# Four weight tiles interleaved column by column, so that the stationary operand is read with a stride of four elements

## The chip, the cores and the metric

The kernel runs on one core of a Trainium2 chip. The metric is the device time of one execution in microseconds (us), lower is better. A difference of 0.2% (4.5 us) is about what a measurement of this kernel can tell from no change.

## The reference

One block of a transformer in float32, for 272 tokens (16 learned "meta" tokens ahead of 256 others), width 2048. Three sublayers are added to the residual stream `h`; the output is `h` without the meta tokens:

```python
h = h + 0.5 * rmsnorm(swiglu(rmsnorm(h), ffn1_w_gu, ffn1_w_down))    # 2048 -> 2 x 5632 -> 2048
h = h + rmsnorm(hybrid_mixer(rmsnorm(h), w_in, pool_w, w_pool_o, w_q_b, w_kv_b, w_mla_o, w_out))
h = h + 0.5 * rmsnorm(swiglu(rmsnorm(h), ffn2_w_gu, ffn2_w_down))
```

The mixer is the sum of two gated branches: window means over the tokens (`w_pool_o`), and attention of 16 heads with low-rank queries, keys and values (`w_q_b`, `w_kv_b`, `w_mla_o`), followed by `w_out`. After the first feed-forward the meta tokens matter as keys, values and window inputs only, so the later products have 256 tokens.

Nearly all of the work is products of an activation with a weight matrix that is used once.

## The kernel before

**Layout.** Activations lie transposed: features on the 128 partitions, tokens along the free dimension. A product is computed as tiles of its transposed output, [128 output features, 272 or 256 tokens] in one PSUM bank: the weight tile [128, 128] is the stationary operand of the tensor engine, and the activation's tile [128, tokens] is the moving one, accumulated over the 128-row tiles `k` of the input (16 of them for width 2048, 44 for 5632).

**Precision.** A float32 is split into two parts of 12 bits, `hi` and `lo`, both of type float32r (4 bytes). A float32 product is made of three products: hi by hi, hi by lo, lo by hi. `mm3` (lines 211 to 215) issues them as three multiplications of 272 or 256 columns: weight `hi` by activation `hi` (L213), weight `hi` by activation `lo` (L214), weight `lo` by activation `hi` (L215). Where there are 256 tokens, `mm_wide` (lines 217 to 221) takes activation `hi` and `lo` side by side: weight `hi` by 512 columns (L219), then weight `lo` by 256 (L221). Each multiplication instruction comes with its own load of the stationary operand (a LDWEIGHTS, shown as PEld), also where L213 and L214 have the same weights.

**The weight stream.** The host lays out all weights as one stream of [128, 128] tiles in the order of their use; the order is collected by a dry run of `build`. In the class `Weights`, `load` (L79) fetches chunks of CH = 8 tiles, [128, 1024] float32, 512 KB, on the SP queue, RAW = 5 chunks ahead. `divide` splits PT = 4 tiles at a time, [128, 512]: ScalarE writes `hi` (L92), VectorE writes `lo` = raw - `hi` (L93), into HL = 6 buffers each. `take` hands out the next tile's `hi` and `lo`: tile `j` of four is the columns `j*128` to `j*128+127` of the [128, 512] buffer, so a weight load reads 128 float32 side by side on each partition.

Only the value projection takes four tiles at once, `take(t0, t1, t2, t3)`: there the activation is the stationary operand and the weights `wh`, `wl` [128, 512] are the moving one (`proj_v`, L603 to L608).

**Stages, in order of time.** First feed-forward (L = 272 tokens, `mm3`; 88 output tiles of 16 `k`, then 16 of 44); the mixer's input product (`mm3`), its 32 gate tiles (`mm_wide`); attention, head by head, with `mm3` of 256 or 272 columns for queries, keys and `w_pool_o` (tiles `q`, `k`, `qr`, `po`), and with multiplications that have no weights (scores `s` L621 and L622, transposes `pt` L653, values `o`); `w_mla_o` with the activation `o`, and `w_out` with the activation `y` (`mm_wide`); the second feed-forward with activations `x` and `a` (`mm_wide`). The last of 16 output tiles of some products is `mm3` with 256 columns. `w<-...` are the first tiles of a product, computed side by side, `m<-...` the rest. `warm` (L232) are multiplications that only keep the tensor engine's clock up; `rms` are those of the norms (L243 with a moving operand of one column; L254 with a stationary operand that is one column repeated 128 times by a stride of zero).

Of the kernel before, what the change touches and what calls it, by code (L numbers as in the profile page):

```python
# [14 lines left out]
P = 128  # L15
# [3 lines left out]
R = 256  # L19
# [8 lines left out]
CH, PT = 8, 4  # L28
RAW, HL = 5, 6
WARM = (3, 7)  # L30
GAP, SPACE = 4, 12

G_F1PRE, G_F1POST, G_MPRE, G_MPOST, G_F2PRE, G_F2POST = (16 * i for i in range(6))
# [5 lines left out]


class Nothing:
    """Stands in for the builder's objects while the order of the weights is collected."""

# [16 lines left out]
class Weights:  # L60
    """The weights as one stream of [128, 128] tiles in the order of their use; each chunk of CH
    tiles is loaded ahead, and split, PT tiles at a time, into two parts of 12 bits, which together
    are the float32."""

# [32 lines left out]
    def take(self, *tiles):  # L97
        """The next tiles of the stream, side by side."""
        n = len(tiles)
        room = PT - len(self.order) % PT  # L100
        if room < n:
            self.order += [None] * room
        at = len(self.order)
        self.order += tiles
        if self.plan is None:
            return Nothing(), Nothing()
        assert self.plan[at : at + n] == list(tiles)
        p, j = divmod(at, PT)
        self.load((p + HL - 1) * PT // CH + RAW)
        self.divide(p + min(HL - 1, p // 2 + 2))  # L110
        for _ in tiles:
            self.tick()
        hi, lo = self.split[p]
        s = slice(j * P, (j + n) * P)
        return hi[:, s], lo[:, s]


class Later:
    """Work that is issued some steps of the weights' stream later, so that an engine isn't held
    by what another one has yet to do."""  # L120

# [3 lines left out]
    def __call__(self, *steps):  # L125
        """steps: pairs of a delay after the one before, and what to run then."""
        at = self.now
        for delay, run in steps:
            at += delay
            self.due.append((at, run))  # L130
        self.due.sort(key=lambda d: d[0])
# [11 lines left out]
def build(nc, tc, ctx, hT, wsrc, gains_d, const_d, tables_d, out, order):  # L143
# [7 lines left out]
    parts = ctx.enter_context(tc.tile_pool(name="parts", bufs=HL))  # L151
# [4 lines left out]
    later = Later()  # L156
# [14 lines left out]

# [1 line left out]
    h = slot3(KD, L, F32, "h")  # L173
# [3 lines left out]
    zero = temp("zero")  # L177
# [5 lines left out]
    ident, ones = const[:, :P], const[:, P:]  # L183
    eps = keep.tile([P, 2], F32, tag="eps", name="eps")
    pool_e.memset(eps[:, 0:1], EPS)
    pool_e.memset(eps[:, 1:2], 4 * EPS)
    acc = keep.tile([P, L], F32, tag="acc", name="acc")
# [6 lines left out]
    class Two:  # L194
        """n tiles of T tokens in two parts of 12 bits, side by side."""

# [20 lines left out]
    def mm_wide(b, w, x, k, first, last):  # L217
        """The same with the product of the low part of x in columns of its own, from R on."""
        mm(b.rearrange("p (b c) -> p b c", b=2), w[0], x.both(k, R), start=first, stop=last,  # L219
           skip_group_check=True)  # L220
        mm(b[:, :R], w[1], x.hi(k, R), start=False, stop=last, skip_group_check=True)  # L221

    def join(b, s):
        """s: the sum of both halves of b, in two steps."""
        act(s, b[:, R:], AF.Copy)
        return GAP, lambda: dve.tensor_tensor(s, b[:, :R], s, op=ALU.add)

    def warm(n, x=ident):
        """Keeps the tensor engine's clock up while it has to wait."""
        b = bank("warm")  # L230
        for _ in range(n):
            mm(b[:, :P], x[:, :P], x[:, :P], start=True, stop=True)  # L232

# [1 line left out]
    def rms_sums(sources, T, n, half=False):  # L235
        """1 / sqrt(mean + eps), or half of it, of the tokens whose squares' sums over the
        partitions of `sources` add up to n * mean; the tokens are on partitions."""
        b = bank("rms")
        tt = (0, P, L - P)[: 3 if T == L else 2]
        m, c0 = len(tt), 400  # L240
        for i, s in enumerate(sources):
            for j, t0 in enumerate(tt):
                mm(b[:, c0 + j : c0 + j + 1], s[:, t0 : t0 + P], ones[:, :1],  # L243
                   start=i == 0 and j == 0, stop=i == len(sources) - 1, skip_group_check=True)
        sd = tmp.tile([P, 4], F32, tag="sd", name="sd", bufs=2)
        f = 4 if half else 1
        act(sd[:, :m], b[:, c0 : c0 + m], AF.Sqrt, scale=f / n, bias=eps[:, f // 4 : f // 4 + 1])
        dve.reciprocal(sd[:, :m], sd[:, :m])
        return b, sd

    def rms_spread(b, sd, T):
        """The same for all partitions, in the bank's first T columns."""
        for j, (t0, c) in enumerate(((0, 0), (P, 0), (L - P, P - NMETA))[: 3 if T == L else 2]):
            mm(b[:, t0 + c : t0 + P], sd[:, j : j + 1].to_broadcast([P, P]), ident[:, c:],  # L254
               start=True, stop=True)
# [8 lines left out]
    def squares(src, T, j, last=False):  # L264
        """Adds the squares of src to acc; the last ones stay apart, for `rms` to add."""
        if j == 0:
            act(acc[:, :T], src, AF.Square)
            return []
        s = temp("sq")
        act(s[:, :T], src, AF.Square)  # L270
        if last:
            return [s]
        pool_e.tensor_tensor(acc[:, :T], acc[:, :T], s[:, :T], op=ALU.add)  # L273
        return []
# [3 lines left out]

# [1 line left out]
    class Stream:  # L280
        """The residual stream's parts for the next products; `update` brings a tile of it up to
        date. Issued in stages that lead the products by a tile."""

# [18 lines left out]
        def scale(self):  # L302
            """The pre-norm's scales; products of the unscaled input are scaled by them."""
            b, sd = rms_sums([acc] + self.last, self.T, DM)

            def spread():
                rms_spread(b, sd, self.T)
                dve.tensor_copy(rs[:, : self.T], b[:, : self.T])
            return spread

    def products(names, n_k, x, T, wave, evac, stream=None, hooks={}, narrow=()):
        """Tiles of x @ w, transposed: the first `wave` of them side by side, then one by one."""
        wide = [T == R and i not in narrow for i in range(len(names))]
# [32 lines left out]

# [1 line left out]
    def post(names, n_k, x, T, g_post, half, wave, wait):  # L348
# [26 lines left out]

# [1 line left out]
    def ffn(x, w_gu, w_down, g_post, wait):  # L377
# [27 lines left out]

    # ================= first feed-forward =================
    warm(10, zero)
# [8 lines left out]

    # ================= mixer =================
    x = advance(t, b, L, G_MPRE)
# [15 lines left out]
    def rotate(o, src, T):  # L434
        """Rotary embedding of rows [x1, x2, x1, x2] of 32 each; o may not be src."""
        c = slice(L - T, L)
# [33 lines left out]
    def windows(j):  # L470
        """Difference of the windows' means and the input, in parts."""
        w = WINDOWS[j // 2]
        s = u[:, j, :]
# [18 lines left out]

    # columns of w_in in tiles: c_kv, k_rope twice, c_q, u_pool
    names = [("w_in", ("kv", j)) for j in range(4)] + [("w_in", ("kr", 0))]
# [57 lines left out]

# [1 line left out]
    o2 = Two(HEADS, R, "o")  # L554
# [40 lines left out]
    def proj_v(g):  # L595
        """Rows of v of four heads: tokens 0.., tokens 128.., and those from 256 on, by the high
        part of the input in rows 64.. and by the low part in rows 80.. ."""
        bs = [bank(f"v{i}") for i in range(3)]
# [47 lines left out]
    def turn(i):  # L646
        """Transposes the probabilities: keys 128.. and keys 0.. of the two times 128 queries. Of
        the first 128 queries' keys from 128 on only 16 exist, the rows below are zero; the second
        ones' keys from 256 on go to rows 64.. and again to rows 80.. of the last columns."""
        b = bank("pt")  # L650
# [49 lines left out]

# [1 line left out]
    y = Two(KD, R, "y")  # L702
# [17 lines left out]

    # ================= second feed-forward =================
    t, b = ffn(advance(t, b, R, G_F2PRE), "ffn2_w_gu", "ffn2_w_down", G_F2POST, (0, 0))
# [15 lines left out]
def columns(name, m):  # L738
    """Columns of a weight that make its tile m."""
    a = np.arange(P)  # L740
# [71 lines left out]
```

## Time and profile before

| | |
|---|---|
| median of 3 runs | 2244.52 us (2244.32 to 2246.24) |
| span of the profiled execution | 2257.5 us |
| PE (multiplications) busy | 99%, 15040 instructions |
| PEld (weight loads) busy | 91%, 15040 instructions |
| VectorE, ScalarE, GpSimd busy | 60%, 51%, 9% |
| DMA | 393.46 MB, mean 174 GB/s |

The profiled execution is 13.0 us longer than the median of the runs. PE's multiplications are pipelined: one begins while the one before it still drains, so the sum of their durations says little, and PE is busy nearly always. What a multiplication takes of PE is read from the distance between the starts of one and the next, that is, from the timeline, or from the count of instructions in a stretch of time. The same holds for PEld.

### The profile page before, as it was taken

To read this page: it belongs to the slowest core of one execution; us is meant where nothing else is said; L and a number is where in the kernel's file an instruction comes from. 1 tells how busy PE (TensorE), PEld (TensorE's weight loads), DVE (VectorE), ACT (ScalarE), POOL (GpSimd) and SP (SyncE) were. 2 spreads that over 40 slices of the span, in tenths; PEclk is the share of its full clock that TensorE was granted. 3 is DMA by queue.
4 is the path that set the end of the run, shared out by engine and by line. 5 is a ranking of instruction groups with operands and counts; after the bars stand their busy time and mean duration, and the time that the engine had idled before them with its cause. 6 is when DMAs were issued, how large, how long until landed. Compare 5 with 4: busy or idle time off the path is not lost.

```text
span 2257.5 us, 39449 instructions
## 1 busy us (share of the span) xinstructions
PE 2234.3 (99%) x15040; PEld 2062.4 (91%) x15040; DVE 1362.2 (60%) x2456; ACT 1142.5 (51%) x2273; POOL 205.4 (9%) x229
## 2 busy tenths in 40 slices
PE   9999999999999999999999999999999999999997
PEld 9999999999999999988888888888888888888886
DVE  6555555555444477766666677577666666654554
ACT  6444444444444454555544555665555555554543
POOL 2000000000000053200121111150000000000001
PEclk9999999999999999999999999999999999999999
DMA  6555555555555545566533356545655555655553
GB/s 242 178 175 174 179 172 178 177 170 177 177 169 180 175 150 168 178 190 188 173 113 122 114 169 195 186 151 186 185 188 184 188 186 186 187 191 187 187 182 117
DMA packets 109311, 393.46 MB, mean 174 GB/s; under 512 B 12288, under 2 KB 13696, under 8 KB 109120
## 3 DMA queue, kind: packets, MB, share of 16 engines
q1 hardware_dynamic: 108576, 389.19, 53.7%
q8 instruction: 118, 1.93, 0.4%
q0 software_dynamic: 400, 1.61, 0.2%
q14 instruction: 73, 0.60, 0.1%
q10 hardware_dynamic: 144, 0.13, 0.0%
HBM read 388.78 MB, written 2.10 MB: 173 GB/s over the span
## 4 chain that ended last, share of the span: by engine, by line
PE 97%; DVE 2%; issue 1%; DMA 0%; ACT 0%; SPq 0%; ACTq 0%; DVEq 0%
PE m L219 29%; PE m L221 15%; PE m L213 13%; PE m L215 12%; PE m L214 12%; PE w L219 2%; PE w L214 1%; PE w L221 1%; PE w L215 1%; PE s L622 1%; PE w L213 1%; PE po L213 1%; PE po L215 1%; PE po L214 1%; PE s L621 1%
## 5 line engine op out<-in xcount | busy, mean ns | idle before, releaser
L93 DVE TENSOR_TENSOR lo<-raw,hi 128x512 fp32r<-128x512 f32 x1472 | 1042.9, 722 | 691.7 <-ACT hi L92 686.7
L92 ACT ACTIVATE hi<-raw 128x512 fp32r<-128x512 f32 x1472 | 882.5, 625 | 393.6 <-PE m L214 283.1
L219 PE MATMUL m<-x,hi 128*128 128x512 f32 x1824 | 643.3, 398 | 0.0
L221 PE MATMUL m<-x,lo 128*128 128x256 f32 x1824 | 513.0, 281 | 0.0
L213 PE MATMUL m<-x,hi 128*128 128x272 f32 (+1 forms) x1488 | 429.6, 289 | 0.0
L215 PE MATMUL m<-x,lo 128*128 128x272 f32 (+1 forms) x1488 | 429.2, 288 | 0.0
L214 PE MATMUL m<-x,hi 128*128 128x272 f32 (+1 forms) x1488 | 428.4, 288 | 0.0
L219 PEld LDWEIGHTS m<-x,hi 128*128 128x128 f32 x1824 | 342.9, 188 | 83.2
L221 PEld LDWEIGHTS m<-x,lo 128*128 128x128 f32 x1824 | 345.0, 189 | 0.0
L214 PEld LDWEIGHTS m<-x,hi 128*128 128x128 f32 x1488 | 282.9, 190 | 0.0
L213 PEld LDWEIGHTS m<-x,hi 128*128 128x128 f32 x1488 | 279.8, 188 | 0.0
L215 PEld LDWEIGHTS m<-x,lo 128*128 128x128 f32 x1488 | 279.7, 188 | 0.0
L219 PE MATMUL m<-a,hi 128*128 128x512 f32 x660 | 233.2, 399 | 0.0
L273 POOL TENSOR_TENSOR acc<-acc,sq 128x272 f32<-128x272 f32 (+1 forms) x88 | 83.4, 948 | 1532.8 <-ACT sq L270 1532.5
L215 PE MATMUL m<-a,lo 128*128 128x272 f32 (+1 forms) x748 | 215.7, 288 | 0.0
L213 PE MATMUL m<-a,hi 128*128 128x272 f32 (+1 forms) x748 | 215.7, 288 | 0.0
L214 PE MATMUL m<-a,hi 128*128 128x272 f32 (+1 forms) x748 | 215.3, 288 | 0.0
L221 PE MATMUL m<-a,lo 128*128 128x256 f32 x660 | 185.4, 281 | 0.0
L219 PEld LDWEIGHTS m<-a,hi 128*128 128x128 f32 x660 | 124.1, 188 | 31.1
L214 PEld LDWEIGHTS m<-a,hi 128*128 128x128 f32 x748 | 142.4, 190 | 0.0
L213 PEld LDWEIGHTS m<-a,hi 128*128 128x128 f32 x748 | 140.8, 188 | 0.0
L215 PEld LDWEIGHTS m<-a,lo 128*128 128x128 f32 x748 | 140.8, 188 | 0.0
(206 smaller groups left out, 2577.4 us busy)
## 6 DMA issues: line engine op xcount, KB each, us to landing
raw<-w SPq DMA_DIRECT2D x735, 512.0 KB, 3.5
h<-hT POOLq DMA_DIRECT2D x4, 272.0 KB, 5.7
out<-t SPq DMA_DIRECT2D x8, 128.0 KB, 1.9
out<-t SPq DMA_DIRECT2D x4, 256.0 KB, 2.1
h<-hT SPq DMA_DIRECT2D x1, 544.0 KB, 9.1
raw<-w SPq DMA_DIRECT2D x2, 256.0 KB, 3.5
MA<-tables POOLq DMA_DIRECT2D x1, 480.0 KB, 3.7
h<-hT SPq DMA_DIRECT2D x2, 136.0 KB, 2.9
```

Source lines behind the costliest of these rows:

```text
L92: nc.scalar.activation(hi, t, AF.Copy)
L93: nc.vector.tensor_tensor(lo, t, hi.bitcast(F32), op=ALU.subtract)
L213: mm(o, wh, xh, start=first, stop=False)
L214: mm(o, wh, xl, start=False, stop=False)
L215: mm(o, wl, xh, start=False, stop=last)
L219: mm(b.rearrange("p (b c) -> p b c", b=2), w[0], x.both(k, R), start=first, stop=last, skip_group_check=True)
L221: mm(b[:, :R], w[1], x.hi(k, R), start=False, stop=last, skip_group_check=True)
L273: pool_e.tensor_tensor(acc[:, :T], acc[:, :T], s[:, :T], op=ALU.add)
L621: mm(b[:, c : c + n], q[:, t0 : t0 + P], k[:, :n], start=True, stop=False)
L622: mm(b[:, c : c + n], qp[hp : hp + 64, t0 : t0 + P], kpe[hp : hp + 64, :n], start=False, stop=True)
```

## The change

The host lays four tiles of the stream (the PT = 4 that are split together) out interleaved: in the [128, 512] buffer, column `c` of tile `j` stands at `4*c + j` and no longer at `128*j + c`. `take` of a single tile hands out a slice with a step of SIDE = 4 elements, so that the load of a stationary operand reads 128 float32 with 16 bytes from one to the next. Tiles that are taken four at a time (the value projection) stay as they were, since they are the moving operand. The DMAs, the splits, the order and the number of the instructions on every engine are the same as before; the changed kernel's sequence of instructions differs from that of before in the line numbers alone.

```diff
+SIDE = 4
...
+def columns_at(j):
+
+    a = j // SIDE * SIDE * P + j % SIDE
+    return slice(a, a + SIDE * (P - 1) + 1, SIDE)
...
     def take(self, *tiles):
...
-        s = slice(j * P, (j + n) * P)
+        s = slice(j * P, (j + n) * P) if n > 1 else columns_at(j)
         return hi[:, s], lo[:, s]
...
-    w = np.zeros((n, P, CH, P), np.float32)
+    w = np.zeros((n, P, CH // PT, PT * P), np.float32)
...
-        w[i // CH, :, i % CH, :] = rows[:, c[0] : c[0] + P] if c[-1] - c[0] == P - 1 and c[64] == c[0] + 64 else rows[:, c]
+        j = i % PT
+        s = slice(j * P, (j + 1) * P) if name == "w_kv_b" and m[0] == "v" else columns_at(j)
+        w[i // CH, :, i % CH // PT, s] = rows[:, c[0] : c[0] + P] if c[-1] - c[0] == P - 1 and c[64] == c[0] + 64 else rows[:, c]
```

## The prediction

> **What bounds the kernel now.** I read the page first, then the chain of waits, then stretches of time, then the timeline of single multiplications. The page:
>
> ```profile
> span 2257.5 us, 39449 instructions
> PE 2234.3 (99%) x15040; PEld 2062.4 (91%) x15040; DVE 1362.2 (60%) x2456; ACT 1142.5 (51%) x2273; POOL 205.4 (9%) x229
> PEclk9999999999999999999999999999999999999999
> PE 97%; DVE 2%; issue 1%; DMA 0%; ACT 0%; SPq 0%; ACTq 0%; DVEq 0%
> ```
>
> PE runs through the whole span at the full granted clock, and 97% of the chain that ended last is PE. So the time is the sum of the distances from one multiplication to the next, and a change elsewhere matters only if PE comes to wait. The change touches nothing but the address pattern of the weight loads (PEld), which run beside the multiplications. The question is what a multiplication costs beyond streaming its columns, and how the weight loads enter into that. Two stretches with one kind of work each, first the `mm3` of 272 columns in the first feed-forward, then the `mm_wide` pairs (512 and 256 columns) in the second (columns: PE, PEld, DVE, ACT, POOL busy, each with its count):
>
> ```profile
> 100.00:500.00 400.00, 400.00 (x3188) 400.00 (x3188) 225.06 (x398) 189.05 (x332) 0.00 (x0) 1.00 0.54 176
> 1600.00:2000.00 400.00, 400.00 (x2265) 347.01 (x2265) 260.51 (x496) 206.63 (x427) 0.00 (x0) 1.00 0.59 185
> ```
>
> 400 us by 3188 is 125.5 ns for a multiplication of 272 columns, 376.4 ns for a triple. 400 us by 2265 is 176.6 ns, 353.2 ns for a pair of 768 columns. Two more stretches, from the timeline: `mm3` of 256 columns, and pairs whose activation is `o`:
>
> ```profile
> 1123.38 0.28 PE L214 MATMUL qr<-CB,hi 128*128 128x256 f32 x1
> ...
> 1126.62 0.28 PE L214 MATMUL po<-Y,hi 128*128 128x256 f32 x1
> ```
>
> ```profile
> 1324.62 0.39 PE L219 MATMUL m<-o,hi 128*128 128x512 f32 x1
> 1324.85 0.28 PE L221 MATMUL m<-o,lo 128*128 128x256 f32 x1
> 1324.97 0.39 PE L219 MATMUL m<-o,hi 128*128 128x512 f32 x1
> ...
> 1358.59 0.39 PE L219 MATMUL m<-o,hi 128*128 128x512 f32 x1
> ```
>
> The first two rows are 27 multiplications apart: 3.24 us by 27 is 120.0 ns, 360.0 for a triple, again 768 columns. Between the first and the last row of the second fence lie 98 pairs: 33.97 us by 98 is 346.6 ns. Same columns, same weights streamed, but three instructions in place of two: one instruction more costs 360.0 - 346.6 = 13.4 ns. So the columns stream at (346.6 - 2 x 13.4) / 768 = 0.4164 ns each, and **every multiplication carries some 13 ns that are not streaming**. The 272 agree: 272 x 0.4164 + 13.4 = 126.7, seen 125.5. And pairs of the same shape take 353.2 with one activation and 346.6 with another, 6.6 ns apart, where only the addresses of the operands differ. The cost beyond streaming thus depends on where the operands lie, which speaks for a clash of two reads of the SBUF.
>
> **The change: the weight loads.** How fast can a load go? With almost nothing to stream, six loads of `warm` tiles, and six whose stationary operand has a stride of zero (rms L254); then the mean duration of such a load and of a normal one:
>
> ```profile
> 807.20 0.75 PEld L232 LDWEIGHTS warm<-const 128*128 128x128 f32 x6
> 807.93 0.74 PEld L254 LDWEIGHTS rms<-const,sd 128*128 128x128 f32 x6
> ```
>
> ```profile
> L213 PEld LDWEIGHTS m<-x,hi 128*128 128x128 f32 x1488 | 279.8, 188 | 0.0
> L254 PEld LDWEIGHTS rms<-const,sd 128*128 128x128 f32 x40 | 5.1, 189 | 0.7 <-DVE sd L248 0.6
> L232 PEld LDWEIGHTS warm<-const 128*128 128x128 f32 x40 | 4.8, 192 | 0.0
> ```
>
> Of six loads in a row, (0.75 - 0.19) / 5 = 112 ns from one to the next; with a stride of zero (0.74 - 0.19) / 5 = 110. So a load's pace is 112 ns for 128 columns, 0.87 ns a column, and it is no faster if all 128 reads hit one place: the pace is that of the columns, not of the memory, as far as these rows go. What no row shows is a stride above one. The load now stays within the same 16 bytes for four columns, 3.5 ns, and moves on to the next 16 bytes then; after the change every column is in another 16 bytes.
>
> The costs beyond streaming go by about this step: 13.4 is 4 x 3.4, and 6.6 is 2 x 3.3. My theory is that the moving read, which goes through its own 16 bytes in 4 x 0.4164 = 1.7 ns, runs into the load's place about four times per load, and is held each time until the load has moved on. With the stride the load stays in a place for 0.87 ns only, a quarter, but passes four times as many. It overtakes the moving read (16 bytes per 0.87 ns against 1.7) where it now lags behind (3.5 against 1.7): the difference of their speeds is 1/0.87 - 1/1.7 = 0.56 per ns against 1/1.7 - 1/3.5 = 0.30 now, so clashes are 1.9 times as frequent, each for a quarter of the time: about half of the cost stays (1.9 / 4 = 0.47).
>
> The sum. How many of each kind there are, with their mean durations:
>
> ```profile
> L219 PE MATMUL m<-x,hi 128*128 128x512 f32 x1824 | 643.3, 398 | 0.0
> L219 PE MATMUL m<-a,hi 128*128 128x512 f32 x660 | 233.2, 399 | 0.0
> L219 PE MATMUL m<-o,hi 128*128 128x512 f32 x224 | 77.7, 391 | 0.0
> L219 PE MATMUL m<-y,hi 128*128 128x512 f32 x144 | 50.9, 399 | 0.0
> L219 PE MATMUL w<-x,hi 128*128 128x512 f32 x96 | 34.8, 405 | 3.6 <-DVE x L298 3.6
> L219 PE MATMUL w<-y,hi 128*128 128x512 f32 x96 | 33.9, 398 | 0.0
> L213 PE MATMUL m<-x,hi 128*128 128x272 f32 x1440 | 416.0, 289 | 0.0
> L213 PE MATMUL m<-a,hi 128*128 128x272 f32 x704 | 203.2, 289 | 0.0
> L213 PE MATMUL w<-x,hi 128*128 128x272 f32 x176 | 51.3, 291 | 0.8 <-ACT hi L92 0.8
> L213 PE MATMUL po<-Y,hi 128*128 128x256 f32 x128 | 37.4, 292 | 0.0
> L213 PE MATMUL q<-CB,hi 128*128 128x256 f32 x64 | 18.1, 283 | 0.0
> ```
>
> These rows hold 3044 pairs, 2320 triples of 272 and 192 of 256; the smaller groups that aren't shown add little and stay out. Beyond streaming, a pair has 353.2 - 319.8 = 33.4 ns, a triple of 272 has 376.4 - 339.8 = 36.6, one of 256 has 360.0 - 319.8 = 40.2. Together 3044 x 33.4 = 101.7 us, 2320 x 36.6 = 84.9, 192 x 40.2 = 7.7: **194 us of the span**. Half of that is 97 us: 2257.5 - 97 = 2160.5 for the profiled execution, and less 13.0 us, by which that one is longer than the median of the runs, 2147.5. I take 2148.
>
> The bounds of this case: at least nothing is saved. At most all of it, but a load can't go below its 112 ns: a pair becomes 512 x 0.4164 + 112 = 325.2 (28.0 saved), a triple of 272 339.8 (36.6 saved, its streaming of 113.3 just covers a load), one of 256 336 (24 saved): 85.2 + 84.9 + 4.6 = 175 us, 2070 by the runs.
>
> The layout costs nothing elsewhere: the same DMAs fetch the same bytes in the same pieces, and the splits go over whole [128, 512] buffers whatever their columns mean. Would they keep up with a faster PE?
>
> ```profile
> L93 DVE TENSOR_TENSOR lo<-raw,hi 128x512 fp32r<-128x512 f32 x1472 | 1042.9, 722 | 691.7 <-ACT hi L92 686.7
> L92 ACT ACTIVATE hi<-raw 128x512 fp32r<-128x512 f32 x1472 | 882.5, 625 | 393.6 <-PE m L214 283.1
> ```
>
> A 4% faster PE lifts VectorE from 60% to 63%; a split of four tiles takes 722 ns on VectorE and feeds four pairs, 1413 ns of PE, or four triples, 1506. There is room.
>
> The Trainium skill, "TensorE: Matmul & The Clock Gate", in "Step-by-step: what each phase is for", says that the loads and the moving operand have read ports of their own, so that a load takes no bandwidth from a running multiplication. By that rule there is no clash to mend, and the sum would be 0. The trace agrees with it so far as the loads are hidden, but pairs of one shape at 346.6 and 353.2 ns don't follow from it.
>
> **The rivals.**
>
> *The load slows down* (ends on the other side). If a load that finds only one column per 16 bytes needs twice the time per column, its 112 ns become 224. It then outlasts the multiplication it hides behind. The point from which it decides: a load beyond 120 ns binds the multiplications of 256 columns, beyond 125.5 ns those of 272. At 224, a triple of 272 becomes 672 (+295.6), one of 256 becomes 672 (+312); in a pair the load of `lo` still hides behind 512 columns (0.23 us between the first two rows of the `o` fence), that of the next `hi` doesn't behind 256 (0.12 us): +104. Sum: 2320 x 295.6 = 686 us, 192 x 312 = 60, 3044 x 104 = 317: +1062 us, 3307. For it: no row shows a strided load, and the slack is only 12 ns. Against: with a stride of zero the load is not faster than with one, so the memory is not what paces it now. At half this slowing (168 ns) it is 2320 x 127.6 + 192 x 144 + 3044 x 48 ns = +470 us, 2714.
>
> The Trainium skill has this rule on the page "SBUF — State Buffer", section "Specifications (TRN2)": the lines have 16 bytes, full bandwidth needs at least two hits on a line, and each step to a new line is paid for. After the change every column is a step to a new line. By how much it slows a load, the page doesn't say, and no run here shows it yet.
>
> *Every fetch of a load takes a slot from the moving read.* If the 13.4 ns are the price of the load's 32 pieces of 16 bytes (0.42 ns each, one column of streaming), 128 pieces cost four times as much, 53.6: +40.2 ns for each of the 2 x 3044 + 3 x 2512 = 13624 multiplications, +548 us, 2792. For it: 32 x 0.4164 = 13.3 fits the measured 13.4 as well as my theory does. Against: pairs of one shape would not differ by 6.6 ns.
>
> *Nothing happens*, as the load reads column by column in either layout and the 13 ns belong to the change of weights. 2244.5. For it: the equal pace at strides zero and one. Against: again the 6.6 ns between equal shapes.
>
> **How the numbers follow.** Faster by my theory: 0.50, from 2070 to 2240. Nothing happens: 0.18, within 4.5 us (0.2%, about what a measurement of this kernel can tell from no change). The load takes slots, or slows by up to a half: 0.14, up to 2792. The load at half its pace: 0.18, 3307. Every slower case together: 0.32. The range must reach from 2070 to 2792 to leave out only the last one: 0.50 + 0.18 + 0.14 = 0.82. It is wide because the price of a strided load has no row; the likeliest case alone is 2070 to 2240, and its number is 2148.
>
> **What the changed profile would show.** If right: PEld's pace where nothing streams unchanged, the count of multiplications in 400 us of the first feed-forward up from 3188 to about 3350 (119.4 ns each), and of the second from 2265 to about 2375; pairs on `o` and on `x` closer together; the multiplications without the new layout (L603 to L608, L621 to L653) as before. If the load is slower: PEld's starts 200 ns and more apart in the `mm3` stretches, and PE waiting on it. If slots are taken: the multiplications themselves longer, by the same amount at 512 and at 256 columns. The prediction is wrong if the 272 stretch shows 125 ns or more for each.

## The result, and the profile after

The changed kernel takes 3508.4 us (median of 4 runs, 3507.5 to 3509.5) against 2244.6: a ratio of 1.563 (95% interval 1.561 to 1.565). The prediction was faster, 2148 us, with a range up to 2792; the time lies far outside it, on the other side.

The page of the changed kernel, the same parts as of before:

```profile
span 3507.8 us, 39449 instructions
PE 3490.8 (100%) x15040; PEld 3463.9 (99%) x15040; DVE 1358.2 (39%) x2456; ACT 1169.7 (33%) x2273; POOL 197.2 (6%) x229
PEclk9999999999999999999999999999999999999999
PE 99%; DVE 0%; DMA 0%; ACT 0%; issue 0%; SPq 0%; ACTq 0%
```

The same instructions, the same clock, and PE still fills the chain. What is new is PEld at 99% (91% before): the weight loads never rest. The same two kinds of stretches, triples in the first feed-forward and pairs in the second:

```profile
200.00:600.00 400.00, 400.00 (x1716) 400.00 (x1716) 122.97 (x216) 103.91 (x180) 0.00 (x0) 1.00 0.28 94
2500.00:2900.00 400.00, 400.00 (x1710) 400.00 (x1710) 208.30 (x394) 168.85 (x342) 18.64 (x19) 1.00 0.42 139
```

400 us by 1716 is 233.1 ns for a multiplication of 272 columns (125.5 before), and by 1710 it is 233.9 ns for one of a pair (176.6 before). Both kinds now have the same pace, whatever they stream. That is the mark of something else setting it, and the loads' own rows say what (L221 and L227 here are L213 and L219 of before, where the mean duration was 188 ns):

```profile
L221 PEld LDWEIGHTS m<-x,hi 128*128 128x128 f32 x1488 | 489.8, 329 | 0.0
L227 PEld LDWEIGHTS m<-x,hi 128*128 128x128 f32 x1824 | 566.4, 311 | 0.0
```

A duration holds a latency too, so the pace is read from the starts. A pair in the timeline:

```profile
2600.03 0.31 PEld L227 LDWEIGHTS m<-x,hi 128*128 128x128 f32 x1
2600.15 0.51 PE L227 MATMUL m<-x,hi 128*128 128x512 f32 x1
2600.25 0.34 PEld L229 LDWEIGHTS m<-x,lo 128*128 128x128 f32 x1
2600.50 0.28 PE L229 MATMUL m<-x,lo 128*128 128x256 f32 x1
2600.51 0.31 PEld L227 LDWEIGHTS m<-x,hi 128*128 128x128 f32 x1
```

A load of `hi` starts at 2600.03, of `lo` at 2600.25, of the next `hi` at 2600.51: two loads in 0.48 us, one behind the other. The multiplication of 512 columns takes 0.51 us in place of 0.40, as one that stands waiting for its weights. (That it is listed from 2600.15, while its load still runs, is no sign of it: the profile of before lists them so too. No view names a wait of PE for PEld either; it is read from the equal paces.) **Every strided load takes about 233 ns from one to the next, where a contiguous one could go at 112, and PE goes at the pace of its loads.**

Both profiles give the size of it. A triple of 272 went from 376.4 to 699.3 ns, one of 256 from 360.0 to 699.3, a pair from 353.2 to 467.8. With the counts of the prediction, 2320 x 322.9 + 192 x 339.3 + 3044 x 114.6 ns = 749 + 65 + 349 = 1163 us; the smaller groups that it left out (64 triples of 272, 172 of 256, 32 pairs) add 83. That is 1246 us, and the span grew by 1250.3.

### The profile page after: what moved, and what is told of

The parts are those of the page before. It is cut to its first block, busy times and chain, and to the rows that moved or that the text cites. A ratio compares the mean times of both kernels' runs of the same rounds, so it can differ in the third digit from the quotient of the medians.

```text
span 3507.8 us, 39449 instructions
## 1 busy us (share of the span) xinstructions
PE 3490.8 (100%) x15040; PEld 3463.9 (99%) x15040; DVE 1358.2 (39%) x2456; ACT 1169.7 (33%) x2273; POOL 197.2 (6%) x229
## 4 chain that ended last, share of the span: by engine, by line
PE 99%; DVE 0%; DMA 0%; ACT 0%; issue 0%; SPq 0%; ACTq 0%
PE m L227 28%; PE m L222 15%; PE m L221 15%; PE m L223 15%; PE m L229 10%; PE w L227 2%; PE w L221 1%; PE w L223 1%; PE w L222 1%; PE po L222 1%; PE po L223 1%; PE po L221 1%; PE w L229 1%; PE s L630 0%; PE q L221 0%; PE k L222 0%
## 5 line engine op out<-in xcount | busy, mean ns | idle before, releaser
L227 PE MATMUL m<-x,hi 128*128 128x512 f32 x1824 | 857.8, 512 | 0.0
L229 PEld LDWEIGHTS m<-x,lo 128*128 128x128 f32 x1824 | 610.9, 335 | 0.0
L222 PE MATMUL m<-x,hi 128*128 128x272 f32 (+1 forms) x1488 | 594.5, 400 | 0.0
L221 PE MATMUL m<-x,hi 128*128 128x272 f32 (+1 forms) x1488 | 590.4, 397 | 0.0
L223 PE MATMUL m<-x,lo 128*128 128x272 f32 (+1 forms) x1488 | 585.3, 393 | 0.0
L227 PEld LDWEIGHTS m<-x,hi 128*128 128x128 f32 x1824 | 566.4, 311 | 0.0
L223 PEld LDWEIGHTS m<-x,lo 128*128 128x128 f32 x1488 | 489.8, 329 | 0.0
L221 PEld LDWEIGHTS m<-x,hi 128*128 128x128 f32 x1488 | 489.8, 329 | 0.0
L222 PEld LDWEIGHTS m<-x,hi 128*128 128x128 f32 x1488 | 489.8, 329 | 0.0
L227 PE MATMUL m<-a,hi 128*128 128x512 f32 x660 | 310.2, 512 | 0.0
L222 PE MATMUL m<-a,hi 128*128 128x272 f32 (+1 forms) x748 | 298.8, 399 | 0.0
L221 PE MATMUL m<-a,hi 128*128 128x272 f32 (+1 forms) x748 | 296.2, 396 | 0.0
L223 PE MATMUL m<-a,lo 128*128 128x272 f32 (+1 forms) x748 | 293.7, 393 | 0.0
L222 PEld LDWEIGHTS m<-a,hi 128*128 128x128 f32 x748 | 246.1, 329 | 0.0
L223 PEld LDWEIGHTS m<-a,lo 128*128 128x128 f32 x748 | 246.1, 329 | 0.0
L221 PEld LDWEIGHTS m<-a,hi 128*128 128x128 f32 x748 | 246.1, 329 | 0.0
L229 PEld LDWEIGHTS m<-a,lo 128*128 128x128 f32 x660 | 221.6, 336 | 0.0
L227 PEld LDWEIGHTS m<-a,hi 128*128 128x128 f32 x660 | 204.6, 310 | 0.0
```

Source lines behind the costliest of these rows:

```text
L221: mm(o, wh, xh, start=first, stop=False)
L222: mm(o, wh, xl, start=False, stop=False)
L223: mm(o, wl, xh, start=False, stop=last)
```

## The experiments

The theories. **A, pieces:** a load pays for each 16 bytes that it touches on a partition, about two columns' time, so that it is slowed as soon as it finds fewer than two columns there. **B, distance:** it pays for the bytes that it steps over. **C:** the prediction's clash of load and moving read. Open too was whether a slow load costs wherever it stands, or only as far as it outlasts the multiplication it runs beside.

**Stride 2.**

```diff
-SIDE = 4
+SIDE = 2
```

> The columns of two tiles interleaved instead of four, so that a stationary operand is read with a stride of two elements (8 bytes) and finds two columns in each 16 bytes. Theory A (pieces: a load takes about twice its time as soon as each column lies in 16 bytes of its own, and not otherwise): loads keep their pace, 120 to 126 ns from one multiplication to the next in the triples, time 2240 to 2250 us. Theory B (distance: the load pays for each byte it steps over, 0 extra at stride 1, about 113 ns extra at stride 4): a third of that at stride 2, some 38 ns for each of 14396 loads where they bind, about 2600 to 2750 us. Theory C (that of the prediction, a clash of the load with the moving read that gets shorter as the load moves on sooner): 2200 us or less.

2268.2 us (2267.4 to 2268.7) against 2244.4, a ratio of 1.010 (1.006 to 1.013). Triples, pairs, and the load's duration:

```profile
100.00:500.00 400.00, 400.00 (x3160) 400.00 (x3160) 223.73 (x395) 187.69 (x330) 0.00 (x0) 1.00 0.53 173
1600.00:2000.00 400.00, 400.00 (x2266) 356.80 (x2265) 260.59 (x496) 205.87 (x426) 0.00 (x0) 1.00 0.58 186
```

```profile
L221 PEld LDWEIGHTS m<-x,hi 128*128 128x128 f32 x1488 | 292.9, 197 | 0.0
```

A load takes 9 ns more (197 against 188), a triple 379.7 in place of 376.4, a pair 353.1 as in the profile of before. B, with its 38 ns a load, is out, and so is C, which needed a gain. A holds, except that it expected no cost at all, and so 2250 us at most. The triples explain 8 of the 24 us. Some 13 more would be the pairs, which were at 353 here, if those of the shorter runs of before go at 347 (below); no run shows that, but the stride is not what makes 353: in the run of patterns (below) pairs at stride 2 took 61 us / 350 x 2 = 348.6.

**The hi parts alone, the lo parts alone.** In the second kernel `hi` and `lo` are exchanged.

```diff
-        return hi[:, s], lo[:, s]
+        c = slice(j * P, (j + n) * P)
+        return hi[:, s], lo[:, c]
```

> The changed layout with the step of four for the hi parts alone; the lo parts are read as 128 columns side by side, which are then those of four tiles, so that the output is not the reference's. Theory A with a chain (a load begins when the multiplication before it begins to stream, a multiplication when its load has ended, so that each multiplication costs the longer of its load, 233 ns strided and 120 contiguous, and its streaming): a triple of 272 takes 233 + 233 + 125 = 591, a pair 233 + 231 = 464, because the strided load of the next hi stands behind 256 columns; time about 3180 us. Rival (a strided load costs its extra wherever it stands, 1250 us by 14396 loads = 87 ns each): 8572 strided loads, +744 us, about 2990 us.

> The mirror image: the step of four for the lo parts alone, hi read contiguous (output not the reference's). Theory A with a chain: a triple of 272 takes 233 + 2 x 125.5 = 484; in a pair the strided load of lo (213 ns) hides behind the 512 columns of hi (231 ns), so pairs stay at 350 to 360; time about 2540 us. Rival (a strided load costs its extra wherever it stands): 5824 strided loads x 87 ns = +506 us, about 2750 us, and pairs at 353 + 117 = 470.

3193.6 us for hi, 2551.6 for lo (one run each). Triples and pairs with strided `hi`, then with strided `lo`:

```profile
200.00:500.00 300.00, 300.00 (x1519) 300.00 (x1518) 108.90 (x191) 91.69 (x158) 0.00 (x0) 1.00 0.34 111
2350.00:2750.00 400.00, 400.00 (x1729) 364.47 (x1728) 201.21 (x378) 161.83 (x324) 0.00 (x0) 1.00 0.44 142
```

```profile
200.00:500.00 300.00, 300.00 (x1864) 300.00 (x1864) 132.68 (x232) 110.78 (x195) 0.00 (x0) 1.00 0.42 136
1900.00:2300.00 400.00, 400.00 (x2267) 400.00 (x2266) 258.58 (x490) 206.58 (x425) 0.00 (x0) 1.00 0.58 187
```

With strided `hi` a triple is 592 ns and a pair 463; with strided `lo` they are 483 and **353, the pair of before**. All four are the sums that were expected of a multiplication that costs the longer of its load and its streaming (591, 464, 484, 350 to 360). The load of `lo` runs beside 512 columns, and there a load of double length is free; that of the next `hi` runs beside 256, and there it isn't. The rival (87 ns for each strided load, wherever) would have had 2990 and 2750 us.

**Other strides in one kernel.** The gate and up tiles take other columns out of the same buffers, in turns of eleven tiles; the first and the last of 16 terms stay contiguous.

```diff
...
+    if how == "s2":
+        a = j // 2 * 256 + j % 2
+        return b[:, a : a + 255 : 2]
+    if how == "s3":
+        return b[:, j : j + 382 : 3]
+    if how == "s4":
+        return b[:, j : j + 509 : 4]
+    if how[0] == "h":
+        n = int(how[1:])
+        return b[:, : 63 * n + 1 : n]
...
```

> The kernel before, with other columns of the split buffers as stationary operands in the gate and up products of both feed-forwards, eleven output tiles of each kind in turn (the products are wrong there, all counts stay). First feed-forward, triples of 272, by kind: stride 1; 2; 3; 4; stride 1 begun two elements (8 bytes) off; then 64 columns only, at stride 1, 4 and 8. Theory A (two columns at least in 16 bytes are free): 376 ns a triple at strides 1 and 2, about 700 at stride 4; at stride 3 (three pieces of 16 bytes for four columns) between, about 540 if a new piece costs a column's time more; off by 8 bytes unchanged; 64 columns at stride 4 and at stride 8 the same, a load of about 107 to 125 ns, so the triple 376 again. Theory B (distance): stride 2 at 484, stride 3 at 590, 64 columns at stride 8 about twice as long as at stride 4. Second feed-forward, pairs, by kind: stride 1 for both 353; hi alone strided 464; lo alone strided 353; both 470; both at stride 3 about 353 to 400; both at stride 2 353; both off by 8 bytes 353; stride 1 353.

Triples at strides 2, 3, 4, and contiguous but 8 bytes off:

```profile
77.00:143.00 66.00, 66.00 (x527) 66.00 (x525) 37.00 (x65) 31.31 (x55) 0.00 (x0) 1.00 0.54 176
144.00:232.00 88.00, 88.00 (x519) 88.00 (x519) 37.55 (x67) 31.41 (x55) 0.00 (x0) 1.00 0.41 131
234.00:348.00 114.00, 114.00 (x517) 114.00 (x518) 36.56 (x64) 31.54 (x55) 0.00 (x0) 1.00 0.31 102
350.00:415.00 65.00, 65.00 (x523) 65.00 (x522) 36.99 (x66) 30.64 (x54) 0.00 (x0) 1.00 0.52 171
```

125.2, 169.6, 220.5 and 124.3 ns a multiplication. Without the two contiguous terms of 16, stride 3 comes to (169.6 - 125.5 / 8) / 0.875 = 176 and stride 4 to 234. Loads of 64 columns only, at strides 1, 4 and 8 (the last column but one is the mean duration):

```profile
L236 PEld LDWEIGHTS m<-x,hi 128*64 128x64 f32 x152 | 20.4, 134 | 0.0
...
L236 PEld LDWEIGHTS m<-x,hi 128*64 128x64 f32 x154 | 29.8, 193 | 0.0
...
L236 PEld LDWEIGHTS m<-x,hi 128*64 128x64 f32 x153 | 30.4, 199 | 0.0
```

Stride 4 costs 59 ns more than stride 1, half of what 128 columns pay. Stride 8, at twice the distance, costs at most 6 more than that. Distance is not what is paid for. And the pieces fit: 128 columns lie in 32 pieces of 16 bytes at stride 1, 64 at stride 2, 96 at stride 3, 128 at stride 4, for paces of 112, under 126, 176 and 234 ns. From 96 on that is 1.83 ns a piece; 64 pieces would be 117, which the streaming of 272 columns covers. The pairs (hi strided, lo strided, both, both at stride 3):

```profile
1630.00:1706.00 76.00, 76.00 (x340) 69.00 (x339) 40.73 (x77) 31.77 (x64) 0.00 (x0) 1.00 0.46 151
1708.00:1769.00 61.00, 61.00 (x349) 60.13 (x348) 40.23 (x77) 31.70 (x66) 0.00 (x0) 1.00 0.56 178
1770.00:1849.00 79.00, 79.00 (x348) 78.08 (x347) 40.75 (x76) 32.83 (x66) 0.00 (x0) 1.00 0.46 147
1850.00:1920.00 70.00, 70.00 (x348) 68.97 (x347) 40.77 (x78) 32.45 (x66) 0.00 (x0) 1.00 0.49 159
```

447.1, 349.6, 454.0 and 402.3 ns, with two contiguous terms of 16 in each; without them (at 353.2 a pair) 460, 349, 468 and 409. Stride 3 had been put at 353 to 400: the miss is mine, since its load of 176 ns outlasts 256 columns too, 231 + 176 = 407.

**The width of the moving operand**, contiguous loads, then strided ones. The first of each sum keeps at least 272 columns, and the paces below hold it too.

```diff
...
+                t = WIDTHS[names[i][0]][i * 8 // len(names)]
+                t = t if k else max(t, L)
...
```

and for the strided kernel, besides:

```diff
-        s = slice(j * P, (j + n) * P)
+        s = slice(j * P, (j + n) * P) if n > 1 else slice(j, j + 509, 4)
```

> The kernel before, with fewer or more moving columns per multiplication in the first feed-forward (the first of each sum keeps at least 272; the products are wrong there): eleven gate and up tiles each of 272, 256, 240, 224, 208, 192, 160 and 128 columns, then two down tiles each of 272, 320, 384, 448, 512, 512, 64 and 32. Chain (a contiguous load and its hand-over take some 120 ns, whatever streams): 126 ns from one multiplication to the next at 272, and 120 flat from 256 down to 32; above 272 the streaming binds, 0.42 ns a column plus 13 to 18 ns: 147 at 320, 174 at 384, 202 at 448, 231 at 512. Rival (13 ns that belong to each multiplication on top of its streaming, the load's own pace being 107 to 112): 120 at 256, 113 at 240, 112 flat from there on down.

> The same widths with each single weight tile read at a step of four elements (on the layout of before, so the products are of mixed columns throughout). Chain: 233 ns flat from 32 to 448 columns, 233 to 240 at 512, where the streaming is as long as the strided load; a strided load is then free. Rival (a strided load slows the moving read as well, or adds its extra to any multiplication): more than 260 ns at 512, and below 233 where there are few columns to stream.

Contiguous, 256, 224, 128, 384 and 512 columns, then 32:

```profile
77.00:139.00 62.00, 62.00 (x523) 62.00 (x522) 36.49 (x65) 30.93 (x55) 0.00 (x0) 1.00 0.54 185
200.00:258.00 58.00, 58.00 (x518) 58.00 (x517) 35.82 (x64) 30.51 (x55) 0.00 (x0) 1.00 0.55 194
437.00:496.00 59.00, 59.00 (x526) 59.00 (x526) 36.44 (x65) 30.12 (x54) 0.00 (x0) 1.00 0.56 196
570.00:614.00 44.00, 44.00 (x253) 44.00 (x252) 14.80 (x22) 13.46 (x23) 0.78 (x1) 1.00 0.38 129
670.00:790.00 120.00, 120.00 (x519) 96.89 (x518) 29.71 (x44) 28.28 (x49) 2.33 (x3) 1.00 0.28 97
845.00:898.00 53.00, 53.00 (x250) 53.00 (x250) 13.77 (x20) 12.57 (x22) 1.26 (x2) 0.50 0.34 119
```

118.5, 112.0, 112.2, 173.9, 231.2 ns, and 212 at 32 columns, where the granted clock (the last column but two) was 0.50. Strided, 256, 128, 272 and 512 columns:

```profile
132.00:255.00 123.00, 123.00 (x526) 123.00 (x526) 37.37 (x65) 31.85 (x55) 0.00 (x0) 1.00 0.27 95
880.00:998.00 118.00, 118.00 (x505) 118.00 (x504) 34.91 (x61) 29.62 (x51) 0.00 (x0) 0.50 0.27 94
1000.00:1060.00 60.00, 60.00 (x259) 60.00 (x258) 15.50 (x24) 16.01 (x27) 0.00 (x0) 0.97 0.28 97
1246.00:1369.00 123.00, 123.00 (x527) 123.00 (x526) 30.11 (x44) 30.08 (x52) 3.09 (x4) 1.00 0.28 95
```

233.8, 233.7, 231.7 and 233.4 ns: flat from 128 to 512 columns. So a strided load costs next to nothing beside 512 columns (233.4 against 231.2), and theory A's chain holds there. Here the buffers have the layout of before, so it is the stride of the read that sets this pace, not what the host laid out. For contiguous loads my expectation of a flat 120 was wrong and the rival right: the floor is 112, the load's own pace (it is no limit on instructions as such: bf16 multiplications of 128 columns, below, came every 55 ns), and 256 columns at 118.5 are above it. What a multiplication of 256 has beyond its streaming is therefore not a wait for its load.

**Bytes or elements, and a strided moving operand.** Blocks of bf16 multiplications ahead of the kernel, and other moving columns in the gate and up tiles.

```diff
...
+    probe(200, z[:, :P], z[:, :512], zb)
...
+    probe(200, z[:, 0:509:4], z[:, :P], zb[:, :P])
...
+            a = (k % 8) * 2 * self.T
+            return self.s2[k // 8][:, a : a + (n - 1) * step + 1 : step]
```

> The kernel before with one weight buffer less, and two additions. First, ahead of everything, blocks of 200 bf16 multiplications (2 bytes, zeros) each with its own load: 512, 256 and 128 moving columns on contiguous stationary columns, then 128 moving columns on stationary columns at strides 2, 4, 6 and 8, then contiguous stationary columns and 256 moving columns at stride 4, 128 at stride 8. If the load's price goes by 16 bytes: strides 2 and 4 (four and two columns in each 16 bytes) at the contiguous pace, stride 6 (three pieces for four columns) and stride 8 (a piece for each) slow, 176 and 233 ns. If it goes by elements: stride 4 already at 233. Second, in the gate and up tiles of the first feed-forward, the moving operand (float32r) with 272 columns, 256 at stride 1 and 2, 128 at stride 1, 2, 3 and 4, and 64 at stride 8 (the products are wrong there). If the moving read pays for pieces of 16 bytes as the load does, at 1.8 ns a piece: 256 at stride 2 (128 pieces) 230 ns or more in place of 119, 128 at stride 4 (128 pieces) 230, 64 at stride 8 (64 pieces) about 117; if a moving read is free of it: 119, and 111, the load's own pace.

Loads of 128 bf16 columns at strides 2, 4, 6 and 8, that is, 4, 8, 12 and 16 bytes (stride 1 has 98 ns as stride 2):

```profile
L424 PEld LDWEIGHTS <-z 128*128 128x128 bf16 x180 | 10.1, 98 | 0.0
...
L424 PEld LDWEIGHTS <-z 128*128 128x128 bf16 x181 | 10.2, 113 | 0.0
...
L424 PEld LDWEIGHTS <-z 128*128 128x128 bf16 x181 | 10.2, 125 | 0.0
...
L424 PEld LDWEIGHTS <-z 128*128 128x128 bf16 x182 | 11.2, 146 | 0.0
```

A bf16 load is shorter from the start (98 ns against 188), and the numbers expected (176, 233) were wrong: it pays 15, 27 and 48 ns at 64, 96 and 128 pieces. It rises from 8 bytes on and is not at its full price at stride 4, so it doesn't go by elements. But the multiplications came every 55 ns up to stride 6 and every 60 at stride 8 (11 us / 183), so a piece costs 0.47 ns at most: the 1.83 ns hold for float32r alone, and for bf16 no law is shown. The moving operand, 256 columns at strides 1 and 2, 128 at strides 1 and 4:

```profile
289.00:351.00 62.00, 62.00 (x523) 62.00 (x522) 36.80 (x65) 30.81 (x55) 0.00 (x0) 1.00 0.57 186
353.00:470.00 117.00, 117.00 (x521) 105.11 (x520) 36.97 (x66) 31.32 (x54) 0.00 (x0) 1.00 0.31 100
471.00:530.00 59.00, 59.00 (x527) 59.00 (x526) 36.18 (x65) 30.66 (x55) 0.00 (x0) 1.00 0.58 188
655.00:716.00 61.00, 61.00 (x516) 61.00 (x515) 36.69 (x66) 30.24 (x54) 0.00 (x0) 1.00 0.57 185
```

118.5 and 224.6 ns (231 without the first of each 16, which keeps 272 columns); 112.0 and 118.2. The moving read of float32r pays double at a stride of 2 already (0.9 ns a column), where a load paid 9 ns in all, and no more than that at a stride of 4 (118.2 by 128 is 0.92). The bf16 block of 256 moving columns at stride 4 pays double too: 44 us / 196 = 224.5 ns against 21 / 194 = 108.2 contiguous. Of the first expectation the 230 at stride 2 came true, the 230 for 128 columns at stride 4 didn't; so neither was right, and the two reads follow different rules. The 64 columns at stride 8 ran at a granted clock of 0.50 and settle nothing.

**Stride 3 everywhere**, as a test of the rule on a number given ahead. The load's 176 ns are taken from the run of patterns; what is tested is how loads and streaming add up.

```diff
-        s = slice(j * P, (j + n) * P)
+        s = slice(j * P, (j + n) * P) if n > 1 else slice(j, j + 382, 3)
```

> Every single weight tile read at a stride of three elements, 12 bytes (mixed columns, so that the output is not the reference's): four columns lie in three pieces of 16 bytes. By the rule that the runs so far give (a load takes 1.8 ns a piece of 16 bytes, or 0.87 ns a column, whichever is more, and 96 pieces 176 ns; a multiplication costs the longer of its load and its streaming): triples of 272 and of 256 at 528, pairs at 231 + 176 = 407; 2384 x 528 + 364 x 528 + 3076 x 407 ns + 143 us for the rest = 2846 us of span, 2833 to 2850 us of time. If the price went by bytes of distance (2 of 3 steps to the price of stride 4): 192 ns a load, 2970 us.

2850.9 us (two runs), 0.9 above the range given, and a span of 2849.3 where the rule gave 2846 (distance: 2970). Triples 400 / 2273 x 3 = 528 as expected, pairs 400 / 1953 x 2 = 410 for 407:

```profile
200.00:600.00 400.00, 400.00 (x2273) 400.00 (x2273) 160.62 (x281) 137.05 (x237) 0.00 (x0) 1.00 0.38 125
2100.00:2500.00 400.00, 400.00 (x1953) 400.00 (x1952) 224.24 (x426) 179.22 (x367) 0.00 (x0) 1.00 0.50 161
```

**Why equal pairs take 347 or 353 ns.** The prediction read this as a matter of addresses. One or three multiplications more ahead of the products of 256 tokens leave the operands' addresses as they were; the PSUM banks of the results move on by one with each of these products, in both kernels alike.

```diff
+        if T == R:
+            warm(1)
         banks = [bank(f"w{i}") for i in range(wave)]
```

> The kernel before with one more multiplication of 128 columns that nothing uses ahead of each of the four products that have 256 tokens throughout. Pairs of the same tensors at the same addresses took 353.3 ns in the second feed-forward of the kernel before and 346.7 there in the run of patterns. If that is a state which the sequence of instructions falls into and keeps, a disturbance can move it: the pairs in w_out or the second feed-forward then change between 346.7, 350.0 and 353.3, and the time by up to 15 us below 2244; if they stay where they were, the time is 2244 to 2247.

> The same with three more in place of one: another disturbance, to see whether the state of the pairs is a matter of chance (it comes out otherwise than with one) or of the tensors (as before). Time between 2229 and 2248 us.

2251.3 us (2250.9 to 2260.8) with one, a ratio of 1.001 (0.999 to 1.003), 2261.1 (2252.3 to 2262.3) with three, 1.002 (1.000 to 1.005): both above what was expected. The same stretch of the second feed-forward, with one more, then with three more:

```profile
1600.00:1900.00 300.00, 300.00 (x1733) 262.39 (x1732) 199.42 (x381) 156.12 (x324) 0.00 (x0) 1.00 0.60 190
```

```profile
1600.00:1900.00 300.00, 300.00 (x1700) 260.30 (x1699) 195.62 (x372) 154.15 (x320) 0.00 (x0) 1.00 0.58 186
```

346.2 and 352.9 ns for the same tensors at the same addresses (the profile of before: 353.2). The run of the widths says it more plainly. Its edit touches the first feed-forward alone; the second is that of the kernel before, instruction by instruction and at the same addresses, with other numbers in the tensors:

```profile
1650.00:2050.00 400.00, 400.00 (x2310) 349.81 (x2309) 266.49 (x507) 208.72 (x434) 0.00 (x0) 1.00 0.56 191
```

346.3 ns where the profile of before has 353.2, and in the last product 346.2 (170 us / 982 x 2) for 352.8. It is a pace that PE falls into and keeps, not a clash of addresses. What chooses it is open. That the added multiplications moved it is not shown: each of the two kernels has two times 9 to 10 us apart, and the profile with one is of a run of the lower time, that with three of the upper.

## Why the prediction was wrong, point by point

**What bounds the kernel**: right. PE sets the time, the DMAs and splits are unchanged and hidden, and nothing but the pattern of the loads matters.

**"Every multiplication carries some 13 ns that are not streaming"**: right in size, but not one amount. With contiguous loads and the prediction's 0.4164 ns a column the widths leave 118.5 - 256 x 0.4164 = 11.9 ns at 256 columns and 231.2 - 213.2 = 18.0 at 512. From these two alone a column takes 0.44 ns, which leaves 6; how much is streaming is open. (bf16 blocks of 512 columns took 33 us / 155 = 213 ns, with nothing over 0.4164 a column.) Wrong is what was made of it.

**"The cost beyond streaming thus depends on where the operands lie"**: the step that failed first. Pairs of 346.6 and 353.2 ns were taken for an effect of addresses; the profile of before and the run of the widths show both at the same addresses, as the two runs with added multiplications do. It was the one observation that spoke for a clash, against the rivals of the slots and of no change and against the rule of the ports, and it carried the chance of 0.50. The sizes that matched (13.4 as 4 x 3.4, 6.6 as 2 x 3.3) were numbers in search of a cause. That a load of four times the pieces leaves 512 columns at 233.4 ns against 231.2 ends the clash, and the rival of stolen slots with it. The Trainium skill, "TensorE: Matmul & The Clock Gate", "Step-by-step: what each phase is for", has read ports of their own for loads and moving operand; this agrees with it. Where the 12 to 18 ns come from stays open.

**"The pace is that of the columns, not of the memory, as far as these rows go"**: true for stride 0 and 1, and of no weight for stride 4. Here the time was decided: the sum left a load at 112 ns, hidden behind 125.5 ns, and at stride 4 it takes 233, which PE then waits for. Strides 0 and 1 both have two columns or more in 16 bytes, so they could not tell the two limits apart. I used the equal pace as an argument against the rival that happened.

**The rival of the slow load** named the mechanism, and its point of decision was right: a load binds as soon as it outlasts the streaming beside it. Its price was too small. The load's pace was taken at 224, twice 112; it is 233.1. That is 27 ns more for each of 2512 triples, 69 us. And in a pair it let the load of `lo` hide and charged 104 ns for that of `hi`; the pair lost 114.6, 32 us more for 3044 of them. That is again the pace, 233.9 for 224, in the load of `hi`; the one of `lo` does hide, as the pair of 353 with `lo` alone strided shows. So in kind it is one term, mis-sized, and 83 us of smaller groups left out: 3307 becomes 3491. Most of the rest is the 13.0 us taken off for the difference of profile and median: that difference seems to be one of the pairs' two paces (last section), and where loads set the pace of the pairs there was none (4 runs within 2.1 us).

**The chances**: 0.18 for this rival, at a number that the range left out by design. The Trainium skill's rule of at least two hits on a line of 16 bytes ("SBUF — State Buffer", "Specifications (TRN2)") was quoted in the prediction as speaking against the change, and it is what the runs show for float32r: strides 1 and 2 nearly free, 3 in between, 4 double. A stated rule that no row contradicts weighed less with me than a mechanism of my own that fitted two numbers.

**The signs**: those named for a slow load came, loads 233 ns apart in the triples and PE at their pace; the 272 stretch shows 233.1 ns, where 125 or more was to mean wrong.

**The cover**: VectorE and ScalarE indeed had room; it was not needed.

## What to carry to other kernels

For float32r operands, keep the stationary columns so dense that each 16 bytes hold at least two of them, a stride of 2 at most, and keep the moving operand contiguous. A slow load costs only what it sticks out beyond the multiplication beside it, so read the price of a load pattern from the shortest moving operand: the same strided load was free beside 512 columns and cost 115 to 122 ns beside 256 or 128. And when a theory rests on two numbers that fit, look first for the run in which the same tensors give the other number.

## What the runs showed of the hardware that was not expected

- A strided load doesn't follow the clock of the array. In the stretch of 128 moving columns the granted clock was 0.50, and the strided loads went on at 233.7 ns (233.8 at 1.00); contiguous ones at that clock (32 columns) took 53 us / 250 = 212 ns, against 112 at full clock.
- A contiguous load took 112 ns for 128 float32 columns at best. The Trainium skill, "TensorE: Matmul & The Clock Gate", "LDWEIGHTS (loading the stationary operand)", gives a load's ns as its columns divided by 1.2; an estimate from that for 128 columns is 106.7. The runs come to about 5% of it for contiguous operands; the strided ones, of which it doesn't speak, take 2.2 times as long.
- The kernel before itself has two times: of 19 runs made beside those with added multiplications, 10 lay at 2244.7 to 2246.3 us and 9 at 2257.4 to 2259.6. The prediction's profile was one of the upper group, which is its distance of 13.0 us to the median; by size that fits the two paces of the pairs (6.6 ns x 2000 = 13 us), though no profile of the lower group was taken. So single executions of this kernel tell only changes above some 15 us from none, and not the 4.5 us named at the start.
